# A hybrid trunk layer on one core: gates written once along rows, and the first row tiles of six groups multiplied before the norm is known

## The chip, the core and the metric

One core of a Trainium2 chip runs the whole program. The metric is device time in microseconds (us), the median of three runs. The engines are TensorE (PE: matmuls; its weight loads are listed as PEld), VectorE (DVE), ScalarE (ACT), GpSimd (POOL) and SyncE (SP, which here only issues DMAs). SBUF is the on-chip memory, PSUM the memory that matmuls accumulate in.

## The reference

One layer on 128 context tokens and 256 latent tokens (T = 384 in all), width 2048. Cut to what the change touches:

```python
def rmsnorm(x, g):
    y = x32 * lax.rsqrt(jnp.mean(x32 * x32, axis=-1, keepdims=True) + EPS)
    return y * g

def adaln(cvec, w_ada, b_ada):                  # one row for context, one for latents
    m = jax.nn.silu(cvec) @ w_ada + b_ada
    return jnp.split(m, 6, axis=-1)             # sh1, sc1, g1, sh2, sc2, g2

def trunk_layer(x, mod, s0_f, s0_b, p):
    sh1, sc1, g1, sh2, sc2, g2 = mod
    h = rmsnorm(x, p['norm_mix']) * (1.0 + sc1) + sh1
    m, s_f, s_b = token_mixers(h, s0_f, s0_b, p)        # starts with z = h @ w_in
    x = x + g1 * m
    h = rmsnorm(x, p['norm_ffn']) * (1.0 + sc2) + sh2
    x = x + g2 * conv_ffn(h, p['w_up'], p['w_conv_ffn'], p['w_down'])
    return x, s_f, s_b
```

The latents get a position embedding first, and a last RMSNorm follows. z has 11 groups of 512 columns.

## The kernel before

Activations lie transposed, features on the 128 partitions and tokens along the row: x is 16 row tiles of 128 x 384, four to an SBUF tile. Every product is made in three matmuls from a high and a low part: `hi*hi + hi*lo + lo*hi` (mm_a, lines 528 to 530; mm_b, lines 533 to 535, with tokens as stationary operand). A weight arrives in chunks of 128 x 1024 (512 KB, tile raw); ACT casts it to whi, DVE subtracts to wlo.

The input projection goes over the 16 row tiles in three rounds (ROUNDS: tiles 0 and 1, 2 to 5, 6 to 15), in each over the 11 groups. Round one leaves its sums in z (slots of 6,144 bytes per partition), later rounds add to it. Two pairs of groups (DUOS: V with GBV, U with DX) have chunks with one row tile of both groups. Between them run the products for adaLN (w_ada; line 468 on PE, or DVE multiply-adds into aacc), whose results land in mods by a transpose and sums (columns). Row tile j of h needs mods of j and the row factor bc1 (one over the root mean square of every token): split_affine multiplies by bc1 on DVE, scales and shifts on ACT, splits in two.

The order on each engine is written at build time by a small planner (Pipe). Chunks are added in PE's order; `early` chunks are loaded first, in that order, the others as buffers come free. Side work are generators (threads) that yield an estimated time or the name of an engine's clock; a step is written out when its time has come and the backlog allows. need_h and finish force steps that a product needs. Each engine then runs its own list in order.

At the start SP loads x0, two small tables, x1 to x3, then weights. input_squares, input_sums and input_norm form bc1 on all four x tiles: squares on ACT, ones times squares on PE (L432), root on ACT, reciprocal on DVE. Then comes the first product (V and GBV, row tile 0). keep_warm puts matmuls on PE that nobody reads.

Later, beside the first part of the up projection (w_up, 8 groups of 8 chunks), two things are written to DRAM by POOL. turn() transposes the residual in four pieces and writes each with sixteen DMAs to turned; ada_mod_dve makes the last gate g2 by quarters and writes each quarter, once per token kind, to gates: eight DMAs, each 128 partitions by 4 values, whose 4-byte values lie 128 values apart. base() reads both back with tokens on partitions, when the last part's down projection starts.

Of the kernel before, what the change touches and what calls it, by code (L numbers as in the profile page):

```python
# [35 lines left out]
DUOS = ((W_V, W_GBV), (W_U, W_DX))  # L36

ROUNDS = ((0, 2), (2, 6), (6, 16))

# [6 lines left out]
START = ((), ((1,), (2,)), ((3, 4), (5, 6), (7,)))  # L46
WARM = (6, 8)
START_DVE = (3,)
# [7 lines left out]
)  # L56
T_DMA = 1.46
TABLES = (AF.Silu, AF.Sigmoid, AF.Gelu_apprx_tanh, AF.Exp, AF.Sqrt)
T_MM = 0.165
# [34 lines left out]
class Pipe:  # L94
# [5 lines left out]
    def __init__(self, nc, pools, look_dma, look_split, backlog):  # L100
        self.nc = nc
        self.V = Engine(nc.vector, self, "d", 0.075, 1.04e-3, 0.52e-3, ("tensor_copy", "tensor_scalar"))
        self.S = Engine(nc.scalar, self, "a", 0.1, 0.83e-3, 0.83e-3, ())
        self.pools = pools
        self.LD, self.LS = look_dma, look_split
        self.backlog = backlog
        self.chunks = []
        self.threads = []
        self.now = 0.0
        self.clock = {"d": 0.0, "a": 0.0, "q": 12.0}  # L110
        self.end = 0.0
# [43 lines left out]
    splits = []  # L155
    hold = True

# [19 lines left out]
    def run_threads(self):  # L177
        for th in list(self.threads):
            own = th[0] in self.splits
            if own and self.hold:  # L180
                continue
            while th in self.threads and th[1] <= self.now and (own or max(self.clock["d"], self.clock["a"]) - self.now < self.backlog):
                self.step(th)
# [11 lines left out]
    def run(self):  # L195
        n = len(self.chunks)
        nxt, ahead, loaded = 0, 0, 0
        for c in sorted((c for c in self.chunks if "early" in c), key=lambda c: c["early"]):
            self.dma(c)
        for i in range(-1, n):  # L200
# [4 lines left out]
            while loaded < n:  # L205
                if "early" in self.chunks[loaded] or self.chunks[loaded].get("spare") is not None:
# [28 lines left out]
def trunk(ctx, tc, a, o):  # L235
# [174 lines left out]

    n1 = {}
# [12 lines left out]

    def input_pairs(i):
        V.tensor_add(n1[i][:, 0:2], n1[i][:, 0:2], n1[i][:, 2:4])

    def input_sums(i):
        if i == 0:
            n1["ps"] = misc("ps_n1")  # L430
        for k in range(2):
            PE.matmul(n1["ps"][:, 0:T], ones, n1[i][:, k], start=i == 0 and k == 0, stop=i == 3 and k == 1)  # L432

    def input_norm():
        v1 = row_tile("v1")
        S.activation(v1, n1["ps"][:, 0:T], AF.Sqrt, bias=eps, scale=1.0 / D)
        V.reciprocal(bc1, v1)

# [46 lines left out]
    def ada_dve(src, key, k2, place, then=None):  # L485
# [31 lines left out]
        return dict(src=src, mm=mm, split=False)  # L517

    def ada_mod_dve(i, q4s):
        def out(q4):  # L520
            for v in range(2):
                G.dma_start(gates[v].rearrange("(m p) -> p m", p=P)[:, 4 * q4:4 * q4 + 4], mods[:, i, 4 * q4:4 * q4 + 4, v])
        return [ada_dve(a["w_ada_dve"][i - 2, q4, k2], (i, q4), k2, [(i, 4 * q4, 4)], (lambda q4=q4: out(q4)) if i == 5 else None)
                for q4 in q4s for k2 in range(8)]
# [25 lines left out]
    def h_slots(i, name):  # L550
        hh[i] = slot(f"{name}h{i}", F32R)
        hl[i] = slot(f"{name}l{i}", F32R)

    h_done, h_queue, h_workers = set(), [], []

    def h_worker():
        while h_queue:
            yield from h_make(h_queue.pop(0))
        h_workers.pop()

    def h_make(j):
        if j % 4 == 0:
            h_slots(j // 4, "h")
        parts = split_affine(x[j // 4][:, j % 4], hh[j // 4][:, j % 4], hl[j // 4][:, j % 4], mods[:, 1, j], mods[:, 0, j], bc1)
        if j == 0:
            yield next(parts)
            pipe.hold = False
            pipe.finish(pipe.splits[0])
        yield from parts
        h_done.add(j)  # L570
# [26 lines left out]

    def win_duo(i, k):
        def mm(c):
            need_h(k + 1)  # L600
            for n, grp in enumerate(DUOS[i]):
                n_acc, width = win_shape(grp)
                if k == 0:
                    z[grp] = slot(f"z{grp}", shape=(P, n_acc, width))
                for m in range(n_acc):
                    t = acc("acc0")
                    s = slice(512 * n, 512 * n + 512)
                    yield win_product(grp, t, m, k, c["hi"][:, s], c["lo"][:, s], True, True)
                    (ev_add if k else ev_first)(z[grp], m, t[:, 0:width])
        return dict(src=a["w_in_1"][i, k], mm=mm)  # L610

    def win_group(grp, rnd, evac):
# [4 lines left out]
        for k0 in range(k_lo, k_hi, 2):  # L617
            def pre(k0=k0):
                if rnd < 2 or grp == 0:
                    need_h(k0 + 2)  # L620
                if rnd == 2 and k0 == k_lo:
                    if grp == 0:
                        mixer_weights()
                    if grp == W_CC:
                        late_constants()
                    if grp == W_H0:
                        mixer_state()

            def mm(c, k0=k0):
                if k0 == k_lo:  # L630
                    accs.extend(acc(f"acc{m}") for m in range(n_acc))
                    if rnd == 0:
                        z[grp] = slot(f"z{grp}", shape=(P, n_acc, width))
                hi = c["hi"].rearrange("p (k n) -> p k n", k=2)
                lo = c["lo"].rearrange("p (k n) -> p k n", k=2)
                for m in range(n_acc):
                    for kk in range(2):
                        yield win_product(grp, accs[m], m, k0 + kk, hi[:, kk], lo[:, kk], k0 + kk == k_lo, k0 + kk == k_hi - 1)
                    if k0 + 2 == k_hi:
                        evac(z[grp], m, accs[m][:, 0:width])  # L640
            out.append(dict(src=a["w_in"][grp, k0 // 2], mm=mm, pre=pre))
# [265 lines left out]
    def rounds(rnd, evac):  # L907
        if rnd:
            return [c for g in range(N_WIN) for c in win_group(g, rnd, evac)]
        out = [c for g in range(N_WIN) if g not in sum(DUOS, ()) for c in win_group(g, rnd, evac)]  # L910
        out.insert(1, win_duo(0, 1))
        out.insert(3, win_duo(1, 1))
        return out

    def make_h(js):
        h_queue.extend(js)
        for _ in range(min(2 - len(h_workers), len(js))):
            h_workers.append(1)
            pipe.spawn(h_worker())

    def ada_first(j):

        place = [(0, j, 1), (1, j, 1)]
        return [dict(ada_pe(a["w_ada_0"][j, k4], (0, -j), 4 * k4, 4, place, lambda: make_h((j,))), spare=-1) for k4 in range(4)]

# [15 lines left out]
    for rnd, (k0, k1) in enumerate(ROUNDS):  # L941
        ada = [c for j2s in START[rnd] for cs in zip(*[two_by_two(j2) for j2 in j2s]) for b in cs for c in b]
        if rnd == 0:
            t0, t1, d0, d1 = ada_first(0), ada_first(1), win_duo(0, 0), win_duo(1, 0)
            for i, c in enumerate(t0 + [d0, t1[0], d1] + t1[1:]):
                c["early"] = i
            side = t0 + [d0] + t1 + [d1]
        else:
            main = rounds(rnd - 1, ev_first if rnd == 1 else ev_add)
            side = merge_streams(main, ada, count(ada) / (len(main) - 1.0))  # L950
        for c in side:
# [161 lines left out]
    def turn():  # L1113

        for q4 in range(4):
# [75 lines left out]
    def base(q4):  # L1191

        pipe.finish(ada_done[5, q4])
        f = slice(512 * q4, 512 * q4 + 512)
# [96 lines left out]

    keep_warm(WARM[0])
    for i in range(4):
        input_squares(i)
        if i:
            input_pairs(i - 1)
            input_sums(i - 1)
    input_pairs(3)
    input_sums(3)
    input_norm()  # L1300
    pipe.chunks[4]["pre"] = lambda: (keep_warm(WARM[1]), need_h(1))
    pipe.run()
# [111 lines left out]
```

## Time and profile before

| | |
|---|---|
| device time, three runs | 1778.97, 1787.3, 1788.08 us |
| median | 1787.3 us |
| profiled execution, device time | 1780.96 us |
| its span, first to last instruction | 1779.2 us |
| mean granted PE clock | 0.994 |
| first product of the input projection | 26.00 us |
| first product of round two | 84.48 us |
| the eight gate writes issued | 757.6 to 942.5 us |
| the 64 turned writes issued | 692.9 to 757.6 us |

The profile is one execution; its times are microseconds from the span's start. A row "x<-y" is an instruction that writes x and reads y; "idle ... <-DVE z" is the time an engine stood still before it and what released it. Matmuls overlap in the pipe, so a matmul of 384 columns lasts 0.33 us and the next starts 0.17 us after it. Stages give busy time per engine, the granted clock as a share of full speed, the busy share of the 16 DMA engines and what they moved. Device time is the span and what lies around it.

### The profile page before, as it was taken

How to read it: one execution, taken by the hardware profiler on the slowest of the kernel's cores; microseconds unless marked ns; L12 is line 12 of the kernel's file. 1: busy time of each engine (PE TensorE's matmuls, PEld its weight loads, DVE VectorE, ACT ScalarE, POOL GpSimd, SP SyncE). 2: the span in 40 equal slices, each digit the busy share in tenths (PEclk: the TensorE clock that was granted, in tenths of full speed). 3: DMA queues.
4: the chain of work that ended last, by engine and by line, in shares of the span. 5: the costliest groups of instructions: out<-in, count | busy, mean ns of one | idle time of the engine just before them, and what ended most of it. 6: DMA issues, size and time to landing. Idle time of an engine off the chain costs nothing.

```text
span 1779.2 us, 26710 instructions
## 1 busy us (share of the span) xinstructions
PE 1741.4 (98%) x10704; PEld 1613.7 (91%) x10704; DVE 1120.3 (63%) x1871; ACT 711.3 (40%) x1074; POOL 72.6 (4%) x118
## 2 busy tenths in 40 slices
PE   8999999999999999998999999999999999999998
PEld 6989889989989989997998889999998899999886
DVE  4595678888986578886975333545543344464656
ACT  5523342234643256343433323434432233443433
POOL 0000000000001002500000000000000000000000
PEclk9999999999999999999999999999999999999999
DMA  8878776576645755776677344443443354434642
GB/s 336 283 286 307 278 255 227 184 245 215 218 131 179 294 209 171 244 189 154 204 164 160 127 128 129 130 126 123 131 127 127 125 166 130 125 125 135 221 140 97
DMA packets 93246, 326.69 MB, mean 184 GB/s; under 512 B 11393, under 2 KB 13697, under 8 KB 93121
## 3 DMA queue, kind: packets, MB, share of 16 engines
q1 hardware_dynamic: 86640, 307.78, 53.8%
q0 software_dynamic: 5760, 16.01, 3.0%
q8 instruction: 84, 1.38, 0.3%
q10 hardware_dynamic: 720, 1.18, 0.2%
q14 instruction: 42, 0.34, 0.0%
HBM read 318.10 MB, written 6.83 MB: 183 GB/s over the span
## 4 chain that ended last, share of the span: by engine, by line
PE 61%; DVE 4%; DMA 4%; ACT 1%; issue 1%; POOL 0%; ACTq 0%; DVEq 0%; POOLq 0%
PE acc L530 13%; PE acc L528 13%; PE acc L529 13%; PE acc L535 7%; PE acc L534 7%; PE acc L533 7%; DMA raw<-in_w_up 4%; DVE aacc L90 1%; DVE wlo L90 1%; DVE glu L90 1%; PE ps_sc L287 0%; DMA xr<-in_xT 0%; ACT whi L90 0%; PE ps_ada L468 0%; DVE xr L90 0%
## 5 line engine op out<-in xcount | busy, mean ns | idle before, releaser
L90 DVE TENSOR_TENSOR wlo<-raw,whi 128x1024 fp32r<-128x1024 f32 x384 | 468.8, 1222 | 502.5 <-ACT whi L90 500.4
L90 ACT CAST whi<-raw 128x1024 fp32r<-128x1024 f32 x384 | 402.9, 1050 | 879.7 <-PE acc L529 380.2
L528 PE MATMUL acc<-h2h,whi 128*128 128x384 f32 x1408 | 473.4, 336 | 9.5 <-ACT whi L90 5.7
L530 PE MATMUL acc<-h2h,wlo 128*128 128x384 f32 x1408 | 472.9, 336 | 2.4 <-DVE wlo L90 2.4
L529 PE MATMUL acc<-h2l,whi 128*128 128x384 f32 x1408 | 472.3, 335 | 0.3
L528 PEld LDWEIGHTS acc<-h2h,whi 128*128 128x128 f32 x1408 | 265.8, 189 | 12.5 <-ACT whi L90 6.7
L530 PEld LDWEIGHTS acc<-h2h,wlo 128*128 128x128 f32 x1408 | 265.7, 189 | 4.3 <-DVE wlo L90 4.3
L529 PEld LDWEIGHTS acc<-h2l,whi 128*128 128x128 f32 x1408 | 265.7, 189 | 0.9 <-DVE h2l L90 0.8
L535 PE MATMUL acc<-whi,gl 128*128 128x512 f32 x528 | 205.5, 389 | 0.0
L534 PE MATMUL acc<-wlo,gh 128*128 128x512 f32 x528 | 205.4, 389 | 0.0
L533 PE MATMUL acc<-whi,gh 128*128 128x512 f32 x528 | 205.4, 389 | 0.0
L528 PE MATMUL acc<-hh,whi 128*128 128x384 f32 x576 | 199.2, 346 | 0.9 <-DVE z L90 0.9
L530 PE MATMUL acc<-hh,wlo 128*128 128x384 f32 x576 | 193.2, 336 | 0.8 <-DVE wlo L90 0.8
L529 PE MATMUL acc<-hl,whi 128*128 128x384 f32 x576 | 192.8, 335 | 0.2 <-DVE hl L90 0.2
L90 DVE SCALAR_TENSOR_TENSOR aacc<-raw,svp,aacc 128x512 f32<-128x512 f32 x270 | 184.7, 744 | 0.0
L90 DVE SCALAR_TENSOR_TENSOR glu<-up,sm,glu 128x127 f32<-128x127 f32 (+1 forms) x352 | 135.3, 414 | 26.7 <-ACT glu L90 20.5
L528 PEld LDWEIGHTS acc<-hh,whi 128*128 128x128 f32 x576 | 108.1, 188 | 11.8 <-issue 7.5
L534 PEld LDWEIGHTS acc<-wlo,gh 128*128 128x128 f32 x528 | 99.1, 188 | 20.7
L535 PEld LDWEIGHTS acc<-whi,gl 128*128 128x128 f32 x528 | 99.1, 188 | 20.5
L533 PEld LDWEIGHTS acc<-whi,gh 128*128 128x128 f32 x528 | 99.1, 188 | 20.4
L530 PEld LDWEIGHTS acc<-hh,wlo 128*128 128x128 f32 x576 | 108.1, 188 | 1.5 <-DVE wlo L90 1.5
L529 PEld LDWEIGHTS acc<-hl,whi 128*128 128x128 f32 x576 | 108.2, 188 | 1.0 <-DVE hl L90 0.4
(175 smaller groups left out, 1610.1 us busy)
## 6 DMA issues: line engine op xcount, KB each, us to landing
raw<-in_w_up SPq DMA_DIRECT2D x176, 512.0 KB, 3.6
raw<-in_w_in SPq DMA_DIRECT2D x88, 512.0 KB, 4.8
raw<-in_w_down SPq DMA_DIRECT2D x88, 512.0 KB, 3.5
raw<-in_w_ada SPq DMA_DIRECT2D x64, 512.0 KB, 5.6
raw<-in_w_ada_dve SPq DMA_DIRECT2D x64, 512.0 KB, 4.5
raw<-in_w_ada_pe SPq DMA_DIRECT2D x64, 512.0 KB, 4.9
raw<-in_w_out SPq DMA_DIRECT2D x32, 512.0 KB, 4.3
x<-in_xT SPq DMA_DIRECT2D x4, 768.0 KB, 7.9
```

The lines of the kernel that those rows point to most:

```text
L90: return f(*args, **kw)
L528: PE.matmul(out, wh, xh, start=first, stop=False)
L529: PE.matmul(out, wh, xl, start=False, stop=False)
L530: PE.matmul(out, wl, xh, start=False, stop=last)
L533: PE.matmul(out, xh, wh, start=first, stop=False)
L534: PE.matmul(out, xh, wl, start=False, stop=False)
L535: PE.matmul(out, xl, wh, start=False, stop=last)
```

## The change

Three things.

*The gate.* All of g2 is copied by DVE to a 128 x 32 tile, turned by one PE transpose to 32 x 128, copied by ACT and written by one DMA of 32 rows of 512 bytes. base() asserts that it has been written.

*The turned writes.* turn() yields after each four DMAs (14.0 by the planner's clock), not after sixteen (12.0).

*Round one.* For six groups (PLAIN: U, DX, CC, CH, CB, H0) the first two row tiles are multiplied without the row factor: `(A x) W` is summed, and the shift `B W` comes from two more columns of the same matmuls (386 columns in place of 384). The sums stay in the same slots of z, the two shift columns in a small tile shifts. When bc1 is known, each of the 24 blocks of z is multiplied by it (fix), and the evacuation in round two adds the shift per token kind (ev_shift: two instructions for one). So the first product needs x0, the first column of w_ada and the first chunk of w_in. x1 to x3 are loaded behind ten weight chunks; their squares are side work, the mean is formed by three small matmuls, a power on POOL, and three matmuls that spread it (as for the second norm before). V and GBV come behind H0 in round one. Warming matmuls are 6 and 3, before 6 and 8. The products of w_ada for round two stand closer to the front of round one (AHEAD).

```diff
+PLAIN = (W_U, W_DX, W_CC, W_CH, W_CB, W_H0)
-WARM = (6, 8)
+WARM = (6, 3)
+AHEAD = (0.0, 3.0, 1.0)
+X_THERE = (5.0, 21.0, 23.5, 26.0)
...
-    load_x(1, x[1], SY)
     S.dma_start(pos, a["pos_c"].rearrange("p k c -> p (k c)"))
-    load_x(2, x[2], SY)
-    load_x(3, x[3], SY)
+    pipe.between = {len_early: lambda: [load_x(i, x[i], SY) for i in range(1, 4)] for len_early in (10,)}
...
     def input_squares(i):
-        add_pos(x[i], i, pos, posr)
-        n1[i] = slot("sq0")
+        if i:
+            add_pos(x[i], i, pos, posr)
+            yield "d"
+        sq = slot("sq0")
         for k in range(0, 4, 2):
-            S.activation(n1[i][:, k:k + 2], x[i][:, k:k + 2], AF.Square)
+            S.activation(sq[:, k:k + 2], x[i][:, k:k + 2], AF.Square)
+            yield "a"
+        V.tensor_add(sq[:, 0:2], sq[:, 0:2], sq[:, 2:4])
+        yield
+        V.tensor_add(sqacc if i == 0 else sq[:, 0], sq[:, 0], sq[:, 1])
+        if i:
+            yield
+            V.tensor_add(sqacc, sqacc, sq[:, 0])
+        squared.append(i)
+    def input_norm():
+        while len(squared) < 4:
+            yield 0.3
+        yield "d"
+        ps = misc("ps_n1")
+        mean_square_rows(ps, sqacc)
+        yield 0.3
+        q = rstd_of(ps, NG, D, "n1")
+        yield 0.9
+        dgs = diags(q)
+        yield
+        bc = misc("ps_bc1")
+        broadcast_rows(bc, dgs)
+        yield 0.2
+        S.copy(bc1, bc[:, 0:T])
+        normed.append(1)
...
+    def rows_of_gate():
+        g = tmp.tile([P, 2, KD], F32, name="gate_v", bufs=1)
+        V.tensor_copy(g, mods[:, 5].rearrange("p m v -> p v m"))
+        yield
+        ps = misc("ps_gate")
+        PE.transpose(ps[0:2 * KD, 0:P], g.rearrange("p v m -> p (v m)"), ident)
+        yield 0.3
+        t = tmp.tile([2 * KD, P], F32, name="gate_r", bufs=1)
+        S.copy(t, ps[0:2 * KD, 0:P])
+        G.dma_start(gates.rearrange("v (m p) -> (v m) p", p=P), t)
...
-        def out(q4):
-            for v in range(2):
-                G.dma_start(gates[v].rearrange("(m p) -> p m", p=P)[:, 4 * q4:4 * q4 + 4], mods[:, i, 4 * q4:4 * q4 + 4, v])
+        def out():
+            pipe.spawn(rows_of_gate())
...
+    def plain_make(j):
+        uh, ul = plain[0][:, j, 0:T + 2], plain[1][:, j, 0:T + 2]
+        A, B, src = mods[:, 1, j], mods[:, 0, j], x[0][:, j]
+        for t0, t1, v in RANGES:
+            S.activation(uh[:, t0:t1], src[:, t0:t1], AF.Copy, scale=A[:, v:v + 1])
+        S.copy(uh[:, T:T + 2], B)
+        yield "a"
+        for t0, t1, v in RANGES:
+            V.scalar_tensor_tensor(out=ul[:, t0:t1], in0=src[:, t0:t1], scalar=A[:, v:v + 1], in1=uh[:, t0:t1].bitcast(F32), op0=ALU.mult, op1=ALU.subtract)
+        V.tensor_sub(ul[:, T:T + 2], B, uh[:, T:T + 2].bitcast(F32))
+        plain_done.add(j)
+    def ev_plain(grp, zt, m, t, add):
+        if add:
+            V.tensor_add(zt[:, m], t[:, 0:T], zt[:, m])
+            V.tensor_add(wb[grp][:, m], t[:, T:T + 2], wb[grp][:, m])
+        else:
+            S.copy(zt[:, m], t[:, 0:T])
+            S.copy(wb[grp][:, m], t[:, T:T + 2])
+    def fix(grp):
+        i = PLAIN.index(grp)
+        while grp not in summed or i and PLAIN[i - 1] not in fixed:
+            yield 0.3
+        for m in range(4):
+            zt = z[grp][:, m]
+            V.tensor_mul(zt, zt, bc1)
+            yield 1.2
+    def ev_shift(grp, zt, m, t):
+        for t0, t1, v in RANGES:
+            V.scalar_tensor_tensor(out=zt[:, m, t0:t1], in0=t[:, t0:t1], scalar=wb[grp][:, m, v:v + 1], in1=zt[:, m, t0:t1], op0=ALU.add, op1=ALU.add)
...
                     G.dma_start(turned.rearrange("(b i) f -> i b f", i=32)[:, :, f:f + 32], t[32 * q:32 * q + 32, i * T:(i + 1) * T].rearrange("p (b j) -> p b j", j=32))
-            yield 12.0
+                yield 14.0
```

How it moves instructions, at three places. First the start, PE's list before, up to the first product (sq are squares of x, ps_n the mean, ps_ada the w_ada products, hh the high part of h):

```order
L423 MATMUL ps_warm<-misc_c 128x256 x6
L432 MATMUL ps_n_140<-sq_129,misc_c 128x384 x2
L432 MATMUL ps_n_140<-sq_136,misc_c 128x384 x2
L432 MATMUL ps_n_140<-sq_147,misc_c 128x384 x2
L432 MATMUL ps_n_140<-sq_157,misc_c 128x384 x2
L468 MATMUL ps_ada<-raw,svp 32x64 x64
L423 MATMUL ps_warm<-misc_c 128x256 x8
L533 MATMUL acc_297<-whi,hh_284 128x512
```

And now (uh and ul are the two parts of x0 scaled and not normed):

```order
L460 MATMUL ps_warm<-misc_c 128x256 x6
L491 MATMUL ps_ada<-raw,svp 32x64 x64
L460 MATMUL ps_warm<-misc_c 128x256 x3
L565 MATMUL acc_257<-uh,whi 128x386
L566 MATMUL acc_257<-ul,whi 128x386
L567 MATMUL acc_257<-uh,wlo 128x386
```

The mean is gone from ahead of the first product. On ACT the squares of x1 to x3 now stand between the casts of the chunks of CH and of CB (z_393 is CC's z, z_477 CH's):

```order
L96 CAST whi<-raw 128x1024
L96 ACTIVATE sq_424<-x_81 128x768
L96 ACTIVATE sq_440<-x_82 128x768
L96 ACTIVATE sq_464<-x_83 128x768
L96 ACTIVATE sq_440<-x_82 128x768
L96 ACTIVATE sq_464<-x_83 128x768
L96 COPY z_477<-acc_473 128x384
L96 COPY shifts<-acc_473 128x2
L96 COPY z_477<-acc_474 128x384
L96 COPY shifts<-acc_474 128x2
```

Five of the six squares are there, ahead of the evacuations of CH. Before, all eight (of x0 to x3) were done before the first cast.

Second, DVE in round two, where the w_ada products of one pair of row tiles run on DVE (aacc). Before:

```order
L90 TENSOR_TENSOR wlo<-raw,whi 128x1024
L90 TENSOR_TENSOR z_296<-acc_1010,z_296 128x512
L90 TENSOR_TENSOR z_296<-acc_1011,z_296 128x512
L90 TENSOR_TENSOR z_296<-acc_1012,z_296 128x512
L90 SCALAR_TENSOR_TENSOR aacc_1042<-raw,svp,aacc_1042 128x512
L90 SCALAR_TENSOR_TENSOR aacc_1043<-raw,svp,aacc_1043 128x512
```

And now (z_393 is CC's z, bc_111 the row factor):

```order
L96 TENSOR_TENSOR wlo<-raw,whi 128x1024
L96 TENSOR_TENSOR z_705<-acc_1077,z_705 128x512
L96 TENSOR_TENSOR z_393<-z_393,bc_111 128x384
L96 TENSOR_TENSOR z_705<-acc_1078,z_705 128x512
L96 TENSOR_TENSOR z_705<-acc_1079,z_705 128x512
L96 SCALAR_TENSOR_TENSOR aacc_1106<-raw,svp,aacc_1106 128x512
L96 SCALAR_TENSOR_TENSOR aacc_1107<-raw,svp,aacc_1107 128x512
```

Multiplications by the row factor stand between evacuations and multiply-adds; from the first aacc row to the last there are six, and U's eight evacuations have become sixteen instructions.

Third, POOL beside the up projection. Before:

```order
L385 TENSOR_TENSOR n_q<-n_r,mhalf 128x3
L1122 DMA turned<-turn 32x12x32 x64
L522 DMA gates<-mods 128x4x1 x8
L1198 DMA gate_14632<-gates 128x2x512
L1199 DMA rows_14631<-turned 128x3x512
```

And now:

```order
L389 TENSOR_TENSOR n_q<-n_r,mhalf 128x3
L1253 DMA turned<-turn 32x12x32 x60
L552 DMA gates<-gate_r 32x128
L1253 DMA turned<-turn 32x12x32 x4
L1329 DMA gate_14735<-gates 128x2x512
L1330 DMA rows_14734<-turned 128x3x512
```

Eight writes of gates have become one, and the last four writes of turned come behind it.

More of the change, by code (lines that the diff above doesn't have):

```diff
@@ L198, in run @@
         for c in sorted((c for c in self.chunks if "early" in c), key=lambda c: c["early"]):
+            if c["early"] in self.between:
+                self.between[c["early"]]()
+                self.clock["q"] += 3 * T_X
             self.dma(c)
@@ L423, in keep_warm @@
             PE.matmul(ps[:, 0:2 * P], ident, misc_c, start=True, stop=True)
[L425 to L437, printed above, removed]
     def columns(ps, n, place):
@@ L552, in h_slots, with need_plain, plain_slot @@
         hl[i] = slot(f"{name}l{i}", F32R)
+    plain, plain_done, wb = [], set(), {}
+    shifts = const.tile([P, len(PLAIN), 4, 2], F32, name="shifts")
+    def plain_make(j):
+        if not plain:
+            plain.extend(slot(n, F32R, (P, 2, 512)) for n in ("uh", "ul"))
+        uh, ul = plain[0][:, j, 0:T + 2], plain[1][:, j, 0:T + 2]
[8 more added lines that the diff above has]
+        plain_done.add(j)
+    def need_plain(n):
+        while not all(k in plain_done for k in range(n)):
+            for th in list(pipe.threads):
+                if th in pipe.threads and th[0] not in pipe.splits + stats:
+                    pipe.step(th)
+    def plain_slot(grp):
+        return slot(f"z{grp}"), shifts[:, PLAIN.index(grp)]
+    def ev_plain(grp, zt, m, t, add):
[5 more added lines that the diff above has]
+            S.copy(wb[grp][:, m], t[:, T:T + 2])
+        if m == 3 and (add or grp not in sum(DUOS, ())):
+            summed.add(grp)
+    def fix(grp):
[6 more added lines that the diff above has]
+            yield 1.2
+        fixed.add(grp)
+    def ev_shift(grp, zt, m, t):
+        for t0, t1, v in RANGES:
+            V.scalar_tensor_tensor(out=zt[:, m, t0:t1], in0=t[:, t0:t1], scalar=wb[grp][:, m, v:v + 1], in1=zt[:, m, t0:t1], op0=ALU.add, op1=ALU.add)
     h_done, h_queue, h_workers = set(), [], []
@@ L596, in win_product, with plain_product, plain_products, win_duo @@
         return 3 * T_MM
-    def win_duo(i, k):
-        def mm(c):
-            need_h(k + 1)
+    def plain_product(out, m, k, hi, lo, first, last):
+        w = slice(m * P, (m + 1) * P)
+        mm_a(out[:, 0:T + 2], hi[:, w], lo[:, w], plain[0][:, k, 0:T + 2], plain[1][:, k, 0:T + 2], first, last)
+        return 3 * T_MM
+    def plain_products(accs, hi, lo):
+        for m in range(4):
+            for kk in range(2):
+                for i in range(2):
+                    PE.matmul(accs[m][:, 0:T + 2], hi[:, kk, m * P:(m + 1) * P], plain[i][:, kk, 0:T + 2], start=kk == 0 and i == 0, stop=False)
+                    yield T_MM
+    def win_duo(i, k, part=None, kept=None):
+        def mm(c):
+            if part == 0:
+                kept.update(hi=c["hi"], lo=c["lo"])
+            if part == 1:
+                c = kept
+            need_plain(k + 1) if DUOS[i][0] in PLAIN else need_h(k + 1)
             for n, grp in enumerate(DUOS[i]):
+                if part not in (None, n):
+                    continue
                 n_acc, width = win_shape(grp)
-                if k == 0:
+                if k == 0 and grp not in PLAIN:
                     z[grp] = slot(f"z{grp}", shape=(P, n_acc, width))
@@ L910, in rounds, with make_h @@
         out = [c for g in range(N_WIN) if g not in sum(DUOS, ()) for c in win_group(g, rnd, evac)]
-        out.insert(1, win_duo(0, 1))
-        out.insert(3, win_duo(1, 1))
+        out[len(PLAIN) - 2:len(PLAIN) - 2] = [win_duo(0, 0), win_duo(0, 1), win_duo(1, 1)]
         return out
-    def make_h(js):
+    def make_h(js, more=0):
         h_queue.extend(js)
-        for _ in range(min(2 - len(h_workers), len(js))):
+        for _ in range(min(2 - len(h_workers), len(js) + more)):
             h_workers.append(1)
@@ L1292, in trunk @@
     keep_warm(WARM[0])
[L1293 to L1301, printed above, removed]
+    add_pos(x[0], 0, pos, posr)
+    for i in range(5):
+        stats.append(input_squares(i) if i < 4 else input_norm())
+        pipe.spawn(stats[i], X_THERE[i] if i < 4 else 0.0)
+    pipe.chunks[4]["pre"] = lambda: keep_warm(WARM[1])
     pipe.run()
```

73 lines of the change are left out of this document (52 added, 21 removed).

## The prediction

> **What bounds the kernel now.** I read the page first, then the table of stages, then the two stretches in which TensorE (PE) is not full.
>
> ```profile
> span 1779.2 us, 26710 instructions
> PE 1741.4 (98%) x10704; PEld 1613.7 (91%) x10704; DVE 1120.3 (63%) x1871; ACT 711.3 (40%) x1074; POOL 72.6 (4%) x118
> ```
>
> PE is the bound: 1779.2 - 1741.4 = 37.8 us of the span is not PE time. So the change can win only what PE loses, and the question is where that lies. The table of stages (start:end, length, PE busy, matmuls, granted clock, DMA share, GB/s) says it:
>
> ```profile
> 26.00:84.48 58.48, 58.33 (x636) 1.00 0.85 305
> 84.48:130.00 45.52, 43.69 (x338) 1.00 0.73 263
> 130.00:200.00 70.00, 70.00 (x702) 1.00 0.84 303
> 757.60:942.00 184.40, 172.55 (x989) 0.96 0.71 182
> ```
>
> Between 26.00 and 84.48 PE is all but full, up to 130 it loses 1.8 us, up to 200 nothing; from 757.6 to 942 it is idle for 11.85 us. The rest is the start, before the first useful matmul at 26.00. The change works on the start and on the stretch behind 757.6.
>
> **The gate writes.** From 757.6 on, POOL issues the eight writes of the gates, two at a time; columns here are start, length, engine, line, operation.
>
> ```profile
> 757.64 1.52 POOL L522 DMA_DIRECT2D gates<-mods  x2
> 814.44 1.54 POOL L522 DMA_DIRECT2D gates<-mods  x2 [55.27 <-DVE mods L90]
> 886.41 1.49 POOL L522 DMA_DIRECT2D gates<-mods  x2 [70.43 <-DVE mods L90]
> 940.97 1.49 POOL L522 DMA_DIRECT2D gates<-mods  x2 [53.07 <-DVE mods L90]
> DMA to landing us min/median/max: 7.2/15.2/16.7
> ```
>
> The 4 us stages behind the second pair:
>
> ```profile
> 820.00:824.00 4.00, 4.00 (x25) 1.00 0.61 31
> 824.00:828.00 4.00, 3.27 (x19) 1.00 0.81 37
> 828.00:832.00 4.00, 1.50 (x6) 1.00 0.73 52
> 832.00:836.00 4.00, 0.44 (x2) 0.52 0.79 275
> ```
>
> The queues are busy (share 0.6 to 0.8) and move 31 to 52 GB/s: 2 KB written in 4-byte pieces holds them for some 15 us, the loads of w_up stand behind, PE runs dry and its clock falls to 0.52. What this costs PE is counted, not read from idle time alone:
>
> ```profile
> L530 PE MATMUL acc<-h2h,wlo 128*128 128x384 f32 x193 | 64.5, 334 | 0.0
> L528 PE MATMUL acc<-h2h,whi 128*128 128x384 f32 x314 | 107.6, 343 | 9.3 <-ACT whi L90 5.7 <-ACT up L90 3.6
> L506 PE MATMUL ps_mod<-aacc,pick 128*32 128x128 f32 x48 | 2.1, 280 | 0.2
> ```
>
> The first row is a quiet stretch, 1100 to 1200: 3 x 193 matmuls in 100 us, 0.173 us each. The others are 757.6 to 942: of the 989 matmuls of that stage 48 are ps_mod, and 941 at 0.173 are 162.8 us; with 2.1 us for ps_mod, plus a restart, some 2.6 us, 184.4 - 162.8 - 2.6 = 19.0 us are lost. The idle 11.85 is part of it, the rest is mostly half clock after the idle.
>
> After the change there is one write of 32 rows of 512 bytes. Its price is not in the trace; the nearest row is that of the turned writes (48 KB each in 128-byte runs), and sixteen of them at 693 and at 726 left PE whole:
>
> ```profile
> sum 56.00, PE 56.00; mean PE 4.00
> DMA to landing us min/median/max: 2.0/4.4/12.5
> ```
>
> (684 to 740 us by fours, and the landing of turned.) So I take 0 for the write, bounds 0 and one gate pair's share, 19.0 / 3 = 6.3 us. Its transpose is one matmul between two products that waits for a DVE copy of 32 columns: like the restart above, 0.5 us (bounds 0.1 and 1). Some of the 19.0 is ordinary (a late wlo, 0.3 to 0.6 us at a time): I keep 17.5 and book **-17.0** for this part (bounds -11 and -19). The turned writes in sixteen groups of four instead of four of sixteen I book at 0: the same writes, thinner.
>
> **The start.** What now stands between the first byte and the first product is shown by the moved bytes (60 us in 40 slices of 1.5 us) and by the chain of before:
>
> ```profile
> GB/s 0 107 355 375 382 372 374 374 395 410 407 412 410 412 410 410 404 404 412 407 412 410 412 399 366 281 38 0 177 328 273 333 281 281 265 330 284 322 303 347
> 9.38 1.43 DVE L90 TENSOR_TENSOR x<-x,posr 128x256 f32<-128x256 f32 x4 [1.77 <-DMA x<-in_xT]
> 20.08 1.99 PE L468 MATMUL ps_ada<-raw,svp 128*32 128x64 f32 x128
> 24.42 0.99 ACT L90 ACTIVATE ht<-ht,mods 128x128 f32<-128x128 f32 x2 [2.72 <-DVE ht L90]
> 26.00 0.50 PE L533 MATMUL acc<-whi,hh 128*128 128x512 f32 x1 [0.28 <-ACT hh L90]
> 32.50 0.25 DVE L90 STREAM_TRANSPOSE tr<-ps_ada 128x64 f32<-128x64 f32 x1 [0.52 <-PE ps_ada L468]
> 33.05 0.16 DVE L90 SCALAR_TENSOR_TENSOR mods<-mods,sm 128x2 f32<-128x2 f32 x1
> L90 ACT COPY z<-acc 128x384 f32<-128x384 f32 x36 | 16.7, 483 | 20.6 <-PE acc L530 20.6
> L90 ACT CAST whi<-raw 128x1024 fp32r<-128x1024 f32 x15 | 15.7, 1053 | 2.2 <-DMA raw<-in_w_in 1.7 <-PE acc L535 0.5
> L90 ACT ACTIVATE sq<-x 128x768 f32<-128x768 f32 x8 | 6.2, 831 | 0.9 <-DVE x L90 0.9
> ```
>
> Before, all four x tiles, their squares and the reciprocal come ahead of 26.00. After, only x0, the first four w_ada chunks and the first w_in chunk do. A weight chunk is 0.524 MB, an x tile 0.786, the small loads 0.64 together. Summing the row: x0, the small loads and x1 are 2.21 MB, reached at 8.5, and DVE has x1 at 9.38, so landing is 0.9 behind. In the new order of SP: first w_ada set 3.53 MB, landed 12.9; w_in of U/DX 14.3; second w_ada set 6.15 MB, 19.4; CC 20.7; then x1 to x3; CH 9.55 MB, 27.7; the next pair of w_ada 10.6 MB, 30.3.
>
> The walk: last 16 matmuls of the first set, a quarter of 1.99, end at 13.4; the columns (32.50 to 33.21) 0.7, 14.1. ACT casts U/DX from 14.3 to 15.4, scales 0.99 and copies two columns (not in the trace; 0.16, as the smallest DVE row) to 16.5: **first product 16.5 instead of 26.00**. The low half follows on DVE at 17.5, the other 11 of U end at 19.4. The second set lands then: 1.99, 21.4; DX 12 x 0.173, 23.5. ACT, in the order shown, copies DX's first block, casts CC (23.65), scales row tile 1 (24.8), DVE its low half (25.6); CC has then 20 products left, 29.1. The pair lands at 30.3 and ends at 30.8. The cast of CH stands behind CC's last copy, 29.8 to 30.9; CH runs to 35.1, the next pair to 36.1. ACT has five squares behind that cast (0.8 each, 34.9), three copies with their two columns (0.57 each, 36.6), then the cast of CB, 37.6: PE waits 1.5 us. By 37.6 it has done 72 products (12.5), the second set (2.0) and two pairs (2.0), so it stands as if it had begun at 21.1 without a gap. Before, it stands as if begun at 26.0 plus 0.15 idle plus 0.4 of slow steps, 26.6. That is 5.5 us.
>
> Of this goes the mean, now made of small matmuls inside CB and H0: the same three and three as for the second norm,
>
> ```profile
> 648.51 0.83 PE L287 MATMUL ps_n<-misc_c,sqacc 128*128 128x1 f32 x6 [0.74 <-DVE sqacc L90]
> 651.56 0.94 PE L287 MATMUL ps_bc<-dg,misc_c 128*128 128x128 f32 x6
> ```
>
> 0.83 + 0.94 = 1.8 us, less what lies under products, 1.7; and 144 products with 386 columns for 384, 0.1. Left: 3.7. The chain between the two (DVE, the power on POOL, the diagonals) took 3.05 us there. Here the first three stand 14 products into CB (40.0), the other three 3 products into H0 (44.1): the products between and a pair cover it; should the sums on DVE come late, PE waits at the first three, and all that is queued behind them.
>
> Then the added work of DVE. Each of 24 blocks is multiplied once by the row factor, and each evacuation of those groups in the second round becomes two instructions:
>
> ```profile
> 88.80:130.00 41.20, 37.56 (x56) 1.00 0.78 280
> L90 DVE SCALAR_TENSOR_TENSOR xr<-acc,mods,xr 128x256 f32<-128x256 f32 x32 | 15.2, 474 | 0.0
> L90 DVE SCALAR_TENSOR_TENSOR xr<-acc,mods,xr 128x128 f32<-128x128 f32 x32 | 11.1, 346 | 12.7 <-PE acc L530 12.6
> L90 DVE TENSOR_TENSOR z<-z,z 128x384 f32<-128x384 f32 x8 | 4.4, 554 | 0.1
> ```
>
> (First row: DVE's own, over the aacc stretch.) There DVE is busy 37.56 of 41.2 and already holds PE up for most of the 1.8 us lost there. In the new order six products (0.55) and the second instruction of eight evacuations (0.474 + 0.346 - 0.55 = 0.27) stand in it: 5.5 us by the rows, some 4.5 with their overlap, for 3.6 free. Bounds for PE are 0 and 4.5 here, and up to 8 with the same work for the four later groups, where DVE has room; I take 2, nearer to the free time. The start is worth 3.7 - 2, **-2** (bounds -6 and +8).
>
> **Sum.** The profiled execution took 1780.96, 1.76 more than its span: 1780.96 - 17.0 - 2 = **1762**. It is the execution near the low end of the three (1778.97 to 1788.08, median 1787.3). I don't add the 6.3 up to the median: behind the first gate pair PE hardly waits in this profile (757 to 785, what PE waited for),
>
> ```profile
> PE acc L530 <- DVE wlo L90: 0.9, 2, 0.6
> ```
>
> so the second and third pair made nearly all of the 19.0, and a run in which the first costs as much would be at 1787 or so. That is a guess; the range holds 6 us above.
>
> **Rivals.** (a) *Half clock at the start.* The clock drops after a gap:
>
> ```profile
> 835.64 0.69 PE L528 MATMUL acc<-h2h,whi 128*128 128x384 f32 x1 [3.56 <-ACT up L90]
> 836.13 0.52 PE L529 MATMUL acc<-h2l,whi 128*128 128x384 f32 x1
> 836.45 0.52 PE L530 MATMUL acc<-h2h,wlo 128*128 128x384 f32 x1
> ```
>
> 0.32 us a product instead of 0.173. In the walk PE has w_ada matmuls in pieces, then gaps of 1 to 2 us, and fewer warming matmuls (9, not 14). At half clock U's 11 products take 1.6 us more, which moves DX, CC and CH: 1764. Against it: each gap is shorter than 3.56. The Trainium skill, "TensorE: Matmul & The Clock Gate", section "What's actually happening", says that the half clock is the default and that it takes about 3.4 us of sustained work to leave it; by that rule this rival would be the likelier. The trace agrees as far as the gap of 3.56 goes; no row shows a PE that is busy half the time. (b) *DVE or ACT eats the start*: the 8 us bound instead of 2, 1768; for it, DVE's 37.56 of 41.2; against, the room behind 130, where PE lost nothing in 70 us. (c) *The start pays in full*, with ACT and DVE hidden: -6, 1758. (d) *The gates were not it*: the loads starve as before behind another transfer, 1779, the same; against it, the dip from 820 on begins with a pair's issue. (e) *Slower: the turned writes.* They now run in sixteen groups from 690 to past 900, beside the aacc loads. Should a group starve w_up like a gate pair, 6.3 us, then from six of sixteen on (38 us over 1762) the kernel is slower, 1800; against it is the PE that stayed whole beside the bursts of sixteen.
>
> **Numbers.** Forecast 0.61, (a) 0.10, (b) 0.12, (c) 0.10, (d) 0.04, (e) 0.03. A measurement tells 0.5%, 9 us, from no change: faster 0.93, same 0.04, slower 0.03. The range 1754 to 1772 holds the forecast, (a), (b), (c) with 4 us each way, and leaves out (d) and (e).
>
> **What would show it.** Right: no stage between 757 and 942 under 100 GB/s for 12 us, PE idle there under 3 us; first product near 16.5; CH's first product near 31; a wait of PE for the cast of CB; the second round beginning 3 to 5 us sooner than 84.48. Wrong: idle of PE behind turned writes or at the gate's transpose; first product behind 19; waits for DVE of more than 5 us between the start of the second round and its end.

## The result, and the profile after

| | before | after |
|---|---|---|
| median, four runs each | 1786.13 us | 1761.37 us |
| lowest to highest | 1778.97 to 1788.08 | 1759.49 to 1762.81 |
| profiled execution, device time | 1780.96 | 1759.49 |
| its span | 1779.2 | 1757.7 |

The ratio of the times is 0.9868, 95% interval 0.9838 to 0.9897: faster by 1.3%. The forecast was 1762, the range 1754 to 1772. Between the two profiled executions lie 21.5 us, 2.5 more than the 19 of the sum.

The page of the changed kernel, first lines (busy time, share, instructions):

```profile
span 1757.7 us, 26828 instructions
PE 1727.9 (98%) x10691; PEld 1605.7 (91%) x10691; DVE 1139.3 (65%) x1944; ACT 715.3 (41%) x1105; POOL 69.0 (4%) x112
```

What PE loses fell from 37.8 to 1757.7 - 1727.9 = 29.8 us. PE's busy time fell too, by 13.5 us: of that, matmuls at half clock are a part (they are longer, so lost time hides in "busy"), and the warming matmuls and the mean, which stood ahead of the first product, another. The same stages as before (start:end, length, PE busy, matmuls, clock, DMA share, GB/s):

```profile
26.00:84.48 58.48, 55.43 (x503) 1.00 0.84 314
84.48:130.00 45.52, 43.08 (x339) 1.00 0.77 273
130.00:200.00 70.00, 70.00 (x699) 1.00 0.83 301
757.60:942.00 184.40, 184.23 (x1073) 1.00 0.66 205
```

The stage behind 757.6 is full now: 1073 matmuls for 989, clock 1.00 for 0.96. The first stage shows 3 us of idle that before did not have: the useful work now begins ahead of 26.00, and meets waits there.

To split the gain, three events are used that both programs have on POOL: the load of the mixing weights (mixw, early in round three), the power of the second norm (n_q), and the first read-back of the gate. POOL's list in time, of the kernel before (start, length, engine, line, operation, idle before it and what ended it):

```profile
193.63 0.88 POOL L345 DMA_DIRECT2D mixw<-in_w_sguT  x1 [192.52 <-PE acc L529]
649.63 0.86 POOL L385 TENSOR_TENSOR n_q<-n_r,mhalf 128x3 f32<-128x3 f32 x1 [78.44 <-DVE n_r L90]
1423.43 0.72 POOL L1198 DMA_DIRECT2D gate<-gates  x1 [480.97 <-PE acc L535]
```

and of the changed kernel, with its one gate write:

```profile
190.77 0.92 POOL L349 DMA_DIRECT2D mixw<-in_w_sguT  x1 [147.12 <-PE acc L566]
646.35 0.87 POOL L389 TENSOR_TENSOR n_q<-n_r,mhalf 128x3 f32<-128x3 f32 x1 [78.45 <-DVE n_r L96]
920.93 0.53 POOL L552 DMA_DIRECT2D gates<-gate_r  x1 [32.52 <-ACT gate_r L96]
1401.41 0.73 POOL L1329 DMA_DIRECT2D gate<-gates  x1 [477.52 <-PE acc L572]
```

In this pair of profiles the start is worth 193.63 - 190.77 = 2.9 us at mixw and 3.3 at the second norm. From the second norm to the read-back before took 773.80, after takes 755.06: the gate part is worth 18.7. Behind the read-back 0.5 is given back: 3.3 + 18.7 - 0.5 = 21.5.

### The profile page after: what moved, and what is told of

Same layout as the page of the kernel before. It is cut to its first block, busy times and chain, and to the rows that moved or that the text cites. A ratio compares the mean times of both kernels' runs of the same rounds, so it can differ in the third digit from the quotient of the medians.

```text
span 1757.7 us, 26828 instructions
## 1 busy us (share of the span) xinstructions
PE 1727.9 (98%) x10691; PEld 1605.7 (91%) x10691; DVE 1139.3 (65%) x1944; ACT 715.3 (41%) x1105; POOL 69.0 (4%) x112
## 4 chain that ended last, share of the span: by engine, by line
PE 68%; DVE 2%; DMA 1%; ACT 0%; issue 0%; POOL 0%; DVEq 0%; POOLq 0%
PE acc L565 15%; PE acc L566 15%; PE acc L567 15%; PE acc L570 7%; PE acc L572 7%; PE acc L571 7%; DMA xr<-in_xT 0%; PE ps_sc L293 0%; PE ps_ada L491 0%; DVE glu L96 0%; DVE aacc L96 0%; DVE wlo L96 0%; DVE xr L96 0%; DMA raw<-in_w_up 0%; PE ps_bc L293 0%
## 5 line engine op out<-in xcount | busy, mean ns | idle before, releaser
L565 PE MATMUL acc<-hh,whi 128*128 128x384 f32 x528 | 182.5, 346 | 2.4 <-DVE z L96 2.4
L567 PE MATMUL acc<-hh,wlo 128*128 128x384 f32 x528 | 177.2, 336 | 0.6 <-DVE wlo L96 0.6
L566 PE MATMUL acc<-hl,whi 128*128 128x384 f32 x528 | 176.7, 335 | 0.0
L565 PEld LDWEIGHTS acc<-hh,whi 128*128 128x128 f32 x528 | 99.1, 188 | 12.4 <-issue 9.6
L567 PEld LDWEIGHTS acc<-hh,wlo 128*128 128x128 f32 x528 | 99.1, 188 | 1.2 <-DVE wlo L96 1.2
L566 PEld LDWEIGHTS acc<-hl,whi 128*128 128x128 f32 x528 | 99.2, 188 | 0.6
```

The source lines that it names most:

```text
L565: PE.matmul(out, wh, xh, start=first, stop=False)
L566: PE.matmul(out, wh, xl, start=False, stop=False)
L567: PE.matmul(out, wl, xh, start=False, stop=last)
```

## The experiments

**The gate alone, and the start alone.** The first kernel is before with the one write of rows; the second is after with this put back:

```diff
-        def out():
-            pipe.spawn(rows_of_gate())
+        def out(q4):
+            for v in range(2):
+                G.dma_start(gates[v].rearrange("(m p) -> p m", p=P)[:, 4 * q4:4 * q4 + 4], mods[:, i, 4 * q4:4 * q4 + 4, v])
...
-                yield 14.0
+            yield 12.0
```

> The kernel before with the gate turned and written by one DMA; start and turned writes as before. Theory (the 4-byte writes hold the queues, w_up waits, PE runs dry): the stretch beside the up projection gets back 17 to 19 us, the second round starts at 84.5 as before, time 1762 to 1765 where before gives 1781. Rival (the loads starve behind the turned bursts or the w_ada loads, and the change of their spacing cured it): at most 5 us gained, 1776 or more. In either case the start gives nothing.

> The changed kernel with the gates written by quarters in 4-byte pieces and the turned writes in bursts, both as before: the new start alone. Theory: second round at 80.9 as in the changed kernel, 3.3 us won up to the second norm, the loss behind the second and third gate pair back; 1776 to 1779 in a run like the profiled one of before, within 0.5% of before. Rival (the new start is worth more than the marks in the trace say, since later stages move with it): under 1772.

The gate alone: 1761.78 us (1760.98 to 1764.58), ratio to before 0.9878 (0.9851 to 0.9904), and PE waits for nothing between 660 and 960. The start alone: 1786.38 (1783.87 to 1791.35), ratio 1.0013 (0.9999 to 1.0027). So the gate carries the gain, as the theory has it. But the start alone came out 7 to 10 us later than expected, although its own marks stand as far ahead as in the changed kernel (mixw at 190.75, the second norm at 646.37). Windows of that kernel, PE alone (stage, length, PE busy, matmuls, clock, DMA share, GB/s):

```profile
755.00:815.00 60.00, 52.88 (x290) 0.91 0.70 164
815.00:855.00 40.00, 31.31 (x182) 0.91 0.78 145
875.00:915.00 40.00, 36.79 (x215) 0.96 0.77 146
```

and the same windows of the kernel before, in its first profile:

```profile
755.00:815.00 60.00, 58.90 (x346) 1.00 0.73 197
815.00:855.00 40.00, 33.04 (x177) 0.91 0.70 144
875.00:915.00 40.00, 36.22 (x203) 0.91 0.79 166
```

PE's idle behind the first pair is 7.1 us here and 1.1 there. From the second norm to the read-back this execution took 782.93 us, 27.9 more than the changed kernel. The loss by the gate writes is not a constant of 19: it differs from one execution to another. By the times the start alone gains nothing that can be measured (ratio 1.0013); whether an earlier start makes the gate pairs dearer, or the difference is chance, is not shown.

**The kernel before, profiled again.** The same program as before, for a second execution.

> The kernel before once more, for a second profile. The prediction guessed that the runs near 1787 are those in which the first gate pair costs PE as much as the second and third did in the first profile (idle of PE 1.1 us in 755 to 815, 6.9 in 815 to 855, 3.8 in 875 to 915). If this execution takes 1784 or more, the guess wants 5 us or more of idle in 755 to 815 and the read-back of the gate 778 or more behind the second norm's power (773.80 there); if it takes 1779 to 1781, about the same as there. Rival: the longer time comes from all three pairs, or from elsewhere in the program.

It took 1795.26 us, the longest of all. Windows, PE alone:

```profile
755.00:815.00 60.00, 51.72 (x294) 0.91 0.77 170
815.00:855.00 40.00, 32.38 (x186) 0.91 0.77 155
875.00:915.00 40.00, 37.97 (x231) 1.00 0.77 155
915.00:942.00 27.00, 23.95 (x119) 0.87 0.64 184
```

and what PE waited for between 660 and 960 (us, times, longest):

```profile
PE acc L528 <- ACT whi L90: 12.9, 2, 8.0
PE acc L528 <- ACT up L90: 7.4, 1, 7.4
```

From the second norm (653.08) to the read-back (1437.73) are 784.65 us, 29.6 over the changed kernel and 10.9 over the first profile. The first window holds 8.3 us of idle for 1.1, which is most of these 10.9; the last window adds 3.1, which the first profile does not have. Another 3.4 us of what this execution took longer lie ahead of the second norm (653.08 for 649.63, with mixw at 193.74 for 193.63), where no gate is written; so much of the rival holds. The guess holds for the gate part of this execution, and the first profile was one with a cheap first pair. What makes the first pair cheap or dear within one program was not found. That the gate writes make most of the spread is seen in the times: kernels with 4-byte writes beside w_up lie between 1778.97 and 1795.26, the changed kernel in eight runs between 1758.96 and 1762.81.

**Length of the pieces, or number and place of the writes?** One kernel writes rows of 512 bytes, but in eight DMAs of 2 KB at the old places; another has the turned writes in bursts of sixteen again.

```diff
+    def rows_of_gate(q4):
...
-        G.dma_start(gates.rearrange("v (m p) -> (v m) p", p=P), t)
+        for v in range(2):
+            G.dma_start(gates[v, 512 * q4:512 * q4 + 512].rearrange("(m p) -> m p", p=P), t[4 * v:4 * v + 4])
```

> The changed kernel with the gate turned and written by quarters: again eight DMAs, two at a time, at the places and with the bytes of before, each now 4 rows of 512 bytes. Theory (the length of the pieces is what costs): as the changed kernel, 1761, up to 1.5 us more for three further transposes; no dip of the moved bytes. Rival (the number of writes, or that they fall between the loads of w_up at these places, is what costs): 5 to 19 us more, PE idle behind the issues.

> The changed kernel with the turned writes in four bursts of sixteen as before. Theory (spreading them is worth nothing): 1761, PE idle between 690 and 942 under 1 us. Rival (the spread protects the loads of w_up): 2 us or more slower, with waits of PE for whi behind the bursts.

The quarters: 1761.34 us (1760.17 to 1762.89), ratio 0.9873 (0.9847 to 0.9899). The stage, and the landing of the writes (times, KB each, median us from issue to landing):

```profile
757.00:942.00 185.00, 184.83 (x1077) 1.00 0.66 205
gates<-gate_r POOLq DMA_DIRECT2D x8, 2.0 KB, 3.1
```

and the first six writes of the kernel before (735 to 900):

```profile
gates<-mods POOLq DMA_DIRECT2D x6, 2.0 KB, 15.8
```

The same bytes in the same number of DMAs at the same places land in 3.1 us and cost nothing; in 4-byte pieces they landed in 15.8. It is the cutting into 4-byte pieces, 512 of them a write in place of 4 rows. (That a write reads 4 partitions now and read 128 before goes with it, and was not tested apart.) The bursts of sixteen: 1761.5 (1759.23 to 1761.85), ratio 0.9869 (0.9839 to 0.99). That edit is worth nothing, and the slower rival dies with it.

**The same 4-byte writes where nobody hurries.** The changed kernel with eight writes of 4-byte pieces, in pairs, from the first w_down stage:

```diff
+    def late_pair(q4):
+        g = tmp.tile([P, 4, 2], F32, name="gate_v")
+        V.tensor_copy(g, mods[:, 5, 4 * q4:4 * q4 + 4])
+        for v in range(2):
+            G.dma_start(gates[v].rearrange("(m p) -> p m", p=P)[:, 4 * q4:4 * q4 + 4], g[:, :, v])
...
+                if part == 0 and k2 == 1:
+                    late_pair(q4)
```

> The changed kernel with the gates written in 4-byte pieces as before, two writes at a time, but in the first w_down stage (behind 942, a pair every 20 us or so) instead of beside the loads of w_up. There the DMA share is 0.36 to 0.44 and PE lost nothing. Theory: a pair costs what the loads behind it can't wait for; it holds the queues for some 15 us here too, but w_down's loads are wanted at half the rate and are ahead: 1760 to 1763, PE full in 942 to 1080. Rival: 4-byte pieces cost 6 to 9 us a pair wherever they stand: 1779 to 1790.

1761.26 us (1760.89 to 1763.5), ratio 0.9859 (0.9844 to 0.9874). The first pair went out at 932, the others at 961, 993 and 1026. The window behind the second pair, and the landing of the writes:

```profile
960.00:980.00 20.00, 20.00 (x90) 1.00 0.56 73
gates<-gate_v POOLq DMA_DIRECT2D x6, 2.0 KB, 16.7
```

They land as late as before, the moved bytes fall to 73 GB/s, and PE stays full. So a pair holds the queues wherever it stands; what it costs depends on the lead of the loads behind it. ACT's casts show the lead: behind the second pair of the kernel before, ACT stood still for 13.0 us ahead of the cast at 828.76, for its load of w_up; here the longest such wait between 942 and 1060 is 5.1 us, and 24 of 30 casts wait for PE, with their load already there. Beside w_up the lead is too little, beside w_down enough.

**What the start is worth in times.** The changed kernel and the gate alone, timed together again.

> The changed kernel itself, timed beside the kernel with the new gates and the old start on the same chip. By the marks of the profiles (mixw issued at 190.77 against 193.90, the second norm at 646.35 against 649.14, the read-back of the gate at 1401.41 against 1404.27) the start is worth 2.8 to 3.1 us, so: 1759 to 1762, and 2.3 to 3.3 below its partner. Rival: what the start wins is given back behind the marks or lies within how executions differ (the first timing put the two at 1761.37 and 1761.78): less than 1 us between them.

> The kernel before with the gate written once along rows, nothing else changed, as its partner: 1762 to 1765 if the start is worth what the marks say, 1760 to 1762 by the rival. Either way without a wait of PE over 1 us between 660 and 960.

1760.45 (1758.96 to 1761.81; ratio 0.9863, 0.9848 to 0.9878) and 1764.57 (1761.44 to 1765.59; ratio 0.9883, 0.9869 to 0.9898): 4.1 us apart, more than was expected, after 0.4 the first time (then in two separate timings). All sixteen runs with new start and row writes (the changed kernel twice, quarters, bursts) have the mean 1761.0, the eight with old start and row writes 1763.2: 2.1 us, with a standard error of 0.7. That is 0.1%. The marks say the same and are no sharper: the second norm's power stands at 646.35, 648.68, 646.57 and 648.73 in the profiles of the first four, at 649.14 and 651.15 in the two of the gate alone, 2.6 us apart in the mean.

**Does the row factor hold up DVE?** The 24 multiplications are taken out:

```diff
-            V.tensor_mul(zt, zt, bc1)
-            yield 1.2
+            yield 0.1
```

> The changed kernel without the 24 multiplications of z by the row factor (that part of the computation is left out; the work they stand between is unchanged). They are 24 x 0.55 = 13 us of DVE. Theory: they cost PE the 0.8 us that the marks lose between the second round's begin (3.6 ahead of before) and mixw (2.9 ahead): mixw at 190.0 instead of 190.77, the time 1 us lower, within the noise of a timing. By the prediction's term (2 us of the 4.5 in the second round): mixw at 188.8. Rival, that DVE eats the start (up to 8 us): 184 to 186, and PE's waits for z gone with it. If the mark does not move, what is lost there has another cause.

1760.46 us (1758.97 to 1762.8). mixw came at 192.91, but the start of this execution was 1.6 us late on its own (the mean's power at 43.42 for 41.84; the group CH ran at half clock from 32.21 on, behind waits of 1.96 and 0.63 us for w_ada), so the distance is compared: from that power to mixw 149.49 us without the multiplications, 148.93 with them. What PE waited for from 84 to 132 in the kernel without them:

```profile
PE acc L565 <- DVE z L96: 2.4, 2, 1.4
PE ps_mod L529 <- DVE aacc L96: 0.3, 1, 0.3
```

The waits for z are the same 2.4 us. Why, DVE's and ACT's lists say; first with the multiplications (the changed kernel):

```profile
100.16 1.05 ACT L96 CAST whi<-raw 128x1024 fp32r<-128x1024 f32 x1 [8.60 <-DMA raw<-in_w_in]
101.23 1.22 DVE L96 TENSOR_TENSOR wlo<-raw,whi 128x1024 fp32r<-128x1024 f32 x1 [2.44 <-ACT whi L96]
```

and without:

```profile
101.69 1.05 ACT L96 CAST whi<-raw 128x1024 fp32r<-128x1024 f32 x1 [9.05 <-DMA raw<-in_w_in]
102.78 1.23 DVE L96 TENSOR_TENSOR wlo<-raw,whi 128x1024 fp32r<-128x1024 f32 x1 [3.21 <-ACT whi L96]
```

DVE stands still there in both, 2.4 and 3.2 us, behind a cast that waits for a load of w_in. The aacc work and the evacuations come out late behind that wait. The multiplications only fill a part of it. The load, in turn, is issued late. SP's rows in the changed kernel, the third being, by the order of the loads, the one that the cast at 100.16 waits for:

```profile
74.21 0.33 SPq L128 DMA_DIRECT2D raw<-in_w_ada  x1
86.85 0.33 SPq L128 DMA_DIRECT2D raw<-in_w_in  x1
94.18 0.37 SPq L128 DMA_DIRECT2D raw<-in_w_in  x1
```

Between the first two SP waits 12.2 us for DVE's aacc, which still reads the buffer that is to be filled (11.8 without the multiplications, 9.4 in the kernel before); the load at 94.18 stands behind one of w_ada that waited 5.2 us in the same way. So DVE does hold up this stretch, but by its multiply-adds and through the buffers. The second instruction of each evacuation stayed in and was not tested.

**Half clock at the start.** Eight profiles have the new start with its warming matmuls. In four of them U's products fell to half clock near 18 us, in four they did not, with the same gaps ahead of them. To have the worst of it, the warming matmuls are taken out.

```diff
-WARM = (6, 3)
+WARM = (0, 0)
```

> The changed kernel without its warming matmuls (18 matmuls whose result nobody reads, ahead of the first product). Of seven profiles with the new start four had U's products at half clock (0.32 us apart) from about 17.9 on and three had not, and the first POOL power came at 42.1 to 42.3 against 41.8. Theory: what half clock costs U lies inside the wait for the pair of w_ada ahead of CH (1.70 us at full clock), so that with half clock from the first product on the power comes at 42 to 43 and the time is unchanged or 1 us higher (1760.5 to 1762.5). Rival (a) of the prediction: U's 12 products take 1.6 us more and all behind them moves: the power at 43.5 to 44, the time 2 us higher.

1762.56 us (1761.21 to 1764.76), ratio 0.9864 (0.9848 to 0.9881); the power at 42.65. Its PE rows: U's second and third matmul, the pair of w_ada ahead of CH, and the first product of round two.

```profile
16.69 0.69 PE L566 MATMUL acc<-ul,whi 128*128 128x386 f32 x1 [0.52 <-DVE ul L96]
17.18 0.53 PE L567 MATMUL acc<-uh,wlo 128*128 128x386 f32 x1
...
30.34 0.64 PE L491 MATMUL ps_ada<-raw,svp 128*32 128x128 f32 x16
...
81.66 0.39 PE L570 MATMUL acc<-whi,hh 128*128 128x512 f32 x1
```

And the same places in the changed kernel, whose U ran at full clock:

```profile
15.72 0.45 PE L565 MATMUL acc<-uh,whi 128*128 128x386 f32 x1 [0.99 <-ACT uh L96]
16.92 0.45 PE L566 MATMUL acc<-ul,whi 128*128 128x386 f32 x1 [0.76 <-DVE ul L96]
...
30.33 0.65 PE L491 MATMUL ps_ada<-raw,svp 128*32 128x128 f32 x16 [1.70 <-DMA raw<-in_w_ada]
31.60 0.64 PE L491 MATMUL ps_ada<-raw,svp 128*32 128x128 f32 x16 [0.63 <-DMA raw<-in_w_ada]
...
38.08 0.45 PE L694 MATMUL acc<-uh,whi 128*128 128x386 f32 x1 [0.39 <-ACT whi L96]
...
80.85 0.39 PE L570 MATMUL acc<-whi,hh 128*128 128x512 f32 x1
```

With U slow the pair starts at 30.34, with U fast at 30.33 after a wait of 1.70: the load sets the time. Round two begins at 80.73 to 80.85 in the three profiles of full kernels with a fast U, at 81.14 to 81.29 in the three with a slow one that load in the same order, at 81.66 here: 0.4 to 0.8 us, not two. This holds for U: in the kernel without the multiplications it was CH, behind that pair, that ran at half clock; no load hid it, and round two began at 82.44, the full 1.6 us later.

**Loading x later.** The two waits for that pair, 2.3 us, look like a gain to be had. Row tiles 1 to 3 of x are loaded behind the pair, and the planner's estimates of when they land (X_THERE) are moved with them:

```diff
...
-            if c["early"] in self.between:
-                self.between[c["early"]]()
-                self.clock["q"] += 3 * T_X
             self.dma(c)
...
                 loaded += 1
+                self.late += 1
+                if self.late == 2:
+                    self.between[10]()
+                    self.clock["q"] += 3 * T_X
```

> The changed kernel with row tiles 1 to 3 of x loaded after CH's first chunk and the first pair of w_ada instead of before them. After the change PE waits 1.70 and 0.63 us for that pair at 30.33 and 31.60, ahead of CH. Theory: the three tiles (2.36 MB, some 5.9 us of transfer) stand in front of the pair, so with the new order the pair comes 5 us sooner, both waits go, the second round begins at 78.5 to 79.0 instead of 80.85, and the time is 2 us lower (0.1%). Rival: the squares and their sums are late instead, and PE waits as long at the mean's first three matmuls (40.83) or for the cast of CB behind them on ACT: the second round at 80.5 to 82, the time unchanged or 1 us higher.

1762.55 us (1759.66 to 1764.56), ratio 0.9874 (0.9859 to 0.9888): no gain, and round two began at 83.75. PE's waits from 10 to 130 (us, times, longest), and ACT's rows ahead of the first:

```profile
PE acc L696 <- ACT whi L96: 3.0, 1, 3.0
PE acc L567 <- DVE z L96: 2.5, 2, 1.8
PE acc L569 <- DVE wlo L96: 1.2, 1, 1.2
```

```profile
37.00 1.65 ACT L96 ACTIVATE sq<-x 128x768 f32<-128x768 f32 x2
38.48 1.10 ACT L96 CAST whi<-raw 128x1024 fp32r<-128x1024 f32 x1
```

The wait for the pair ahead of CH is gone; in its place PE waits 3.0 us for CB's cast, which stands on ACT behind two squares of x that came late. In this execution U ran at half clock too, with no wait left to hide it. The rival was right, and its price was higher than it said; how much of that is the half clock was not separated.

## Why the prediction was right, step by step

- *What bounds it.* Right: PE's loss lay in the two stretches, and both gave.
- *The gate, -17.0.* The mechanism is right and shown (the gate alone, the quarters). The size was 18.7: the 1.5 us kept back as ordinary waits are gone too, for the stage (757 to 942) now holds PE for 184.83 of 185 us, and the 0.5 for the transpose was not paid. The write itself at 0 was right. But 19.0 was the loss of one execution; others lost 27.9 and 29.6. (The landing of 15.2 that the prediction read is a median over the eight writes and the four later read-backs of the gate.)
- *The spread.* The guess that dear runs are those with a dear first pair held in both executions profiled besides (8.3 and 7.1 us of idle for 1.1). So the forecast, made from the cheapest of the three profiled, met a median that lies 25 us below the median of before. That it lies within 0.6 us of this median is in part luck: between the two profiled executions 21.5 us were won, where the sum had 19, the gate and the start each a little too small.
- *The walk.* First product at 15.72 for 16.5; the w_ada behind U at 19.06, DX at 20.99; the pair at 30.33 for 30.3. CH began at 32.17, not 30.9: the second half of the pair came 1.3 us after the first, which the walk let land at once. So PE reached CB later and waited 0.39 for its cast, not 1.5. The two errors cancel: round two began 3.6 us sooner (84.48 and 80.85), the walk had 3.7.
- *DVE in round two, 2 us.* Mis-sized, and the larger part of its reason fell. The marks lose 0.8 between there and mixw, and taking out the multiplications gives nothing back: DVE stands idle there behind a load of w_in, which waits for a buffer that DVE's multiply-adds hold. The first row of that part, DVE busy 37.56 of 41.2, is an average that does not show this. The bound of +8 for the start is DVE's 8 us without the 3.7 they are set against; rival (b) has it as 1768, which is +4.3.
- *The turned writes, 0.* Right.
- *Rival (a), half clock.* For U its condition was met in half of the profiles, and the argument against it does not hold: each gap was shorter than 3.56, here at most 1.0 us, and half clock came all the same. Its price was 0.4 to 0.8 us, because the next load hides the rest; for CH it was the full 1.6. (b), DVE or ACT eating the start, and (c), the start paid in full, lie on the two sides of the 2.9 that mixw shows; (d) and (e) fell by the gate alone and by the bursts.
- *What would show it.* No stage from 757 to 942 stays under 100 GB/s for 12 us: single stages of 4 us fall to 8 and 12 GB/s, with the queues idle (share 0.03 and 0.04); in this stretch SP waits 74 us for wlo and 57 for aacc to free a buffer, so it is not the queues that hold the loads back. Idle of PE there is 0.2 us, and its waits for DVE in round two are 2.4 us, under the 5.

## What to carry to other kernels

When the queues are busy and move little, look for a transfer in small pieces nearby; judge its price by the lead of the loads behind it, since the same writes were free 100 us later. A loss that hangs on such timing belongs to an execution, so take a second profile before sizing it. A step that leaves the front of the program is worth no more than the next transfer allows: here two waits of 1.7 and 0.6 us, and moving the load turned them into one of 3.0.

## What the runs showed that was not expected

The clock differs between executions of the same instructions. Windows of PE from 17 to 19 us, with the clock behind the matmul count, first the changed kernel, then the kernel with the gate in quarters, whose start is the same:

```profile
17.00:19.00 2.00, 2.00 (x11) 1.00 1.02 410
```

```profile
17.00:19.00 2.00, 2.00 (x8) 0.62 1.02 410
```

The Trainium skill, "TensorE: Matmul & The Clock Gate", section "What's actually happening", says that activity is judged in a free-running window and that the number of slow matmuls varies from run to run. The runs agree: 1.00 and 0.62 after gaps that are the same within 0.05 us.

How a wait is divided matters as well. In round two PE waits for z at two places, 1.53 and 0.82 us in the profiled changed kernel, and goes on at full clock. In its second profile there was one wait:

```profile
111.88 0.66 PE L565 MATMUL acc<-hh,whi 128*128 128x384 f32 x1 [2.70 <-DVE z L96]
112.33 0.52 PE L566 MATMUL acc<-hl,whi 128*128 128x384 f32 x1
112.65 0.52 PE L567 MATMUL acc<-hh,wlo 128*128 128x384 f32 x1
```

The products behind it are 0.32 us apart, and from the mean's power to mixw this execution took 151.39 us for 148.93: a wait of about the same sum cost 2.5 us more. Of the nine profiles with the new start three have one wait there (1.84, 2.19 and 2.70 us), and half clock follows in each; six have two waits, none over 1.77, and stay at full clock. Nine profiles make no rule, and at CH two waits of 1.96 and 0.63 were enough.
